# Moving the operands of TensorE's products to another place in SBUF: 192 bytes, by 256, from the stationary ones

## The chip, the cores and the metric

One core of a Trainium2 chip runs the whole model: TensorE (matmul), VectorE, ScalarE, GpSimd and SyncE (DMA queue), with SBUF (128 partitions of on-chip memory) and PSUM (where products add up). The metric is the device time of one execution in microseconds, the median of several runs.

## What is computed

Two transformer layers, then one block of another kind, on 256 tokens of 1024 features, in float32. Cut to its dense products, the reference is:

```python
x = x + concat(attention(h), mamba2(h)) @ out_w          # h = rmsnorm(x) @ in_w, split
x = x + (silu(h @ w_gate) * (h @ w_up)) @ w_down         # swiglu, D_FF = 2816
x = x + (gate_b * causal_conv(gate_c * v)) @ out_w       # short convolution, 1024 wide
x = x + (silu(h @ w_gate) * (h @ w_up)) @ w_down
x = rmsnorm(x)
x = x + (sigmoid(ga) * (y_a @ w_a) + sigmoid(gb) * (y_b @ w_b)) @ w_out   # second block
x = x + peer_ffn(rmsnorm(x), wq, sub_keys, u, v)
# peer_ffn: per token and head the 16 best of 128 x 128 experts; hid = gelu(u[expert] . x) * gate; sum of hid * v[expert]
```

The kernel computes `peer_ffn` densely: the hidden values of all 16384 experts (`u`, 128 chunks), a mask of gates, and the sum over all of them (`v`, 128 chunks).

## The kernel before

**Weights.** All weights come from HBM as a stream of 537 chunks of 128x1024 float32 (`Stream`): SyncE loads `raw` (three buffers), ScalarE writes its rounded part `whi` and VectorE the rest `wlo` (`cut`, lines 75 and 76), four buffers each, at most three chunks ahead of TensorE. The activations are split in the same way: `hh` and `hl` are h, and each stage has such a pair of its own (`yh` and `yl` and so on, by `split2`).

**Products.** One dense product is three instructions with the same output (`mm3`, lines 283 to 285), high by high, high by low, low by high. Each reads a stationary 128x128 tile, loaded into the array ahead of it, and a moving operand of 256 or 512 columns. In the profile's names the moving operand stands first: `w<-hh,whi` has hh moving and whi stationary. `gemm_b` has a chunk stationary and h moving, 24 products for one output; `gemm_o` has a chunk stationary and a pair y moving, each product of three going to the next of eight outputs; `gemm_a` has h stationary and the chunk moving, 512 columns wide as a rule.

**Stages, in order of time.** `mixer0` (the first 190 us), `ffn`, `short_conv`, `ffn`, `mixer2` (from about 660 us to 880), `peer` (the rest). In `peer` the products with `u` (`gemm_b`, to about 1290 us) run beside the search for the 16 best on VectorE and then beside one half of the gates (products of 64 columns, line 1616); the last stage, 128 chunks of `v`, runs beside the other half. There `part` splits two 128-row blocks of the hidden values at a time into h's own memory, and h is stationary. Between stages `enter` writes h anew. Work of VectorE and ScalarE that is not due at once stands in a list (`later`), and `run` issues it between the products, by credits, so its order on each engine is fixed when the program is written.

**Places in SBUF.** A place is an address within a partition; "by 256" is its remainder. Tiles lie one behind the other in the order of the pools: constants, the stream (raw, whi, wlo), `res` (xT, hh, hl), small, and each stage's own pool, in steps of 32 bytes. Before the change:

| tile | used by | place | by 256 |
|---|---|---|---|
| whi, wlo (four each, 4096 apart) | all | 31200, 47584 and on | 224 |
| xT | all | 63968 | 224 |
| hh, hl | all | 72160, 80352 | 224 |
| yah, yal | mixer0 | 203104, 207200 and on | 96 |
| ybh, ybl | mixer0 | 219552, 223648 and on | 160 |
| yh, yl | the first ffn | 108672, 112768 and on | 128 |
| yh, yl | short_conv | 110784, 115904 and on | 192 |
| yh, yl | the second ffn | 120960, 125056 and on | 128 |
| yah, ybh, mgh and their low parts | mixer2 | 207232, 203136, 215424 and on | 128 |

Within a tile, the blocks that a product reads lie 512 or 1024 bytes apart, so a product's remainder is its tile's. Moving less stationary, by 256, is then: h against the stream 0, in either role; mixer0's ya 128 (96-224) and yb 192; the FFNs' y 160; the short convolution's y 224; mixer2's ya, yb and mg 160. SBUF is nearly full: the highest place in use is 228063 of 229376.

Of the kernel before, what the change touches and what calls it, by code (L numbers as in the profile page):

```python
# [7 lines left out]
F32 = mybir.dt.float32  # L8
F32R = mybir.dt.float32r
# [109 lines left out]
class Kernel:  # L119
# [30 lines left out]
    def start(self):  # L150
        nc = self.nc
        c = self.const
        self.xT = self.res.tile([128, 8, 256], F32, name="xT")
        self.cols = self.a["cols"]
        self.g = c.tile([128, self.a["gains"].shape[1]], F32, name="gains")
        nc.scalar.dma_start(self.g, self.a["gains"])
        self.after = nc.scalar.dma_start(self.xT[:, 0:2], self.a["xT"][:, 0:2]).ins
        self.ones = c.tile([128, 128], F32, name="ones")
        nc.vector.memset(self.ones, 1.0)
        with self.tc.issue_after(self.after):  # L160
            a = nc.scalar.activation(c.tile([128, 1], F32, name="first"), self.ones[:, 0:1], AF.Copy)
        jp = self.jp = c.tile([128, 128], I32, name="jp")
        nc.gpsimd.iota(jp, pattern=[[1, 128]], base=0, channel_multiplier=-1)
        self.ident = c.tile([128, 128], F32, name="ident")
        v = nc.vector.tensor_scalar(self.ident, jp, 0.0, None, op0=OP.is_equal)
        self.idle = self.side([128, 128])
        self.spin(12)
        self.after = a.ins, v.ins
# [47 lines left out]
            v.tensor_mul(t, t, a)  # L216
            v.scalar_tensor_tensor(y, t, 1.5, y, op0=OP.add, op1=OP.mult)

    def parts(self, name="h"):
        return (self.res.tile([128, 8, 256], F32R, name=name + "h"), self.res.tile([128, 8, 256], F32R, name=name + "l"))  # L220

    def add(self, accs):

# [213 lines left out]
    def short_conv(self, h):  # L437
        nc, w, st = self.nc, self.work, self.st
        rsb = accs = None
        ys = []  # L440
        ahead = None

        def banks(bank=self.bank):
            return bank([128, 2, 256]), bank([128, 256])

        for b in range(8):
            cv, gb = ahead or banks(self.side if b == 0 else self.bank)
            if b == 0:
                self.gemm_b3([(cv[:, 0], True), (cv[:, 1], False), (gb, True)], h)
                rs = self.held(self.stats)()  # L450
                ahead = banks()
                for i in range(2):
                    self.gemm_b(ahead[0][:, i], h, st.next(), i == 0)
                self.gemm_b(ahead[1], h, st.next(), True)
                rsb = self.held(lambda: self.bcast_rs(rs))()
                accs = self.accs()
            else:
                if ahead is None:
                    for i in range(2):
                        self.gemm_b(cv[:, i], h, st.next(), i == 0)  # L460
                    self.gemm_b(gb, h, st.next(), True)
                ahead = None
            u = w.tile([128, 258], F32, name="u")
            nc.gpsimd.memset(u[:, 0:2], 0.0)
            t = w.tile([128, 256], F32, name="t")
            nc.vector.tensor_mul(t, cv[:, 0], rsb)
            nc.gpsimd.tensor_mul(t, t, rsb)
            nc.vector.tensor_mul(u[:, 2:258], cv[:, 1], t)
            c = w.tile([128, 256], F32, name="c")
            self.conv(c, u, [self.col("l1_conv", 8 * k + b) for k in range(3)], None)  # L470
            g = w.tile([128, 256], F32, name="gb")
            nc.vector.tensor_mul(g, gb, rsb)
            nc.vector.tensor_mul(c, c, g)
            ys.append(self.split2(c, w, "y", [128, 256], 5))
            if b >= 3:
                self.gemm_o(accs, ys[b - 3], st.next(), b == 3, False)
        self.gemm_o(accs, ys[5], st.next(), False, False)
        self.gemm_o2(accs, ys[6:])
        return accs
# [27 lines left out]
    def mixer0(self, h):  # L507
        nc, w, st, a = self.nc, self.work, self.st, self.a
# [4 lines left out]
        def t1(shape, name, dtype=F32, bufs=1, tag=None):  # L513
            return w.tile(shape, dtype, name=name, tag=tag or name, bufs=bufs)
# [3 lines left out]
        p = self.side([128, 256])  # L518
# [16 lines left out]
        for i, f in enumerate((lambda k: key(k), lambda k: latent(c1, k), lambda k: key(k), lambda k: latent(c1, k),  # L535
                               lambda k: key(k), lambda k: key(k), lambda k: latent(c2, k), lambda k: latent(c2, k))):
            k = (0, 0, 2, 2, 4, 6, 4, 6)[i]
# [101 lines left out]
        self.run(1)  # L639


        cs = t1([128, 2, 256], "cs")
        for tb in range(2):
            S.activation(cs[:, tb], cps[tb], AF.Copy, scale=rs[:, tb:tb + 1])
        cn = (t1([128, 2, 256], "cnh", F32R), t1([128, 2, 256], "cnl", F32R))
# [97 lines left out]
        for b in range(2):  # L743
            p = wbank([128, 2, 256])
# [7 lines left out]
        for tb in range(2):  # L752
            p = wbank([128, 512])
# [124 lines left out]
        MM, yy = {}, {}  # L878
# [18 lines left out]
        def ssd(tb, g):  # L897
            def f():
                o = slice(512 * g, 512 * g + 512)
                p = self.side([128, 512])  # L900
                for j in range(2):
                    m = MM.pop((tb, g, j))
                    for i in range(4):
                        hh = 4 * j + i
                        T.matmul(p[:, hh * 64:hh * 64 + 64], m[:, i], xdt[:, tb, 512 * g + hh * 64:512 * g + hh * 64 + 64],  # L905
                                 start=True, stop=True)
                y = t1([128, 512], "yy", bufs=1)
                if tb:
                    p2 = self.side([128, 512])
                    T.matmul(p2, bcT[:, 2 + g, 128:256], state[:, g], start=True, stop=True)  # L910
                    V.tensor_tensor(y.rearrange("p (h d) -> p h d", d=64), p2.rearrange("p (h d) -> p h d", d=64),
                                    eacs[:, 8 * g:8 * g + 8][:, :, None].to_broadcast([128, 8, 64]), op=OP.mult)
                    V.tensor_add(xsd[:, tb, o], xsd[:, tb, o], y)
                V.tensor_add(xsd[:, tb, o], p, xsd[:, tb, o])
            return f
# [3 lines left out]
        def gate1(tb, g):  # L919
            def f():  # L920
                o = slice(512 * g, 512 * g + 512)
                y = xsd[:, tb, o]
                V.tensor_mul(y, y, zs[:, tb, o])
                sq = t1([128, 512], "ysq", bufs=1, tag="yy")
                S.activation(sq, y, AF.Square, accum_out=yss[:, g, tb:tb + 1])
            return f

# [69 lines left out]
        for k in range(12):  # L997
# [3 lines left out]
            y = yaT[k // 2] if k < 4 else ybT[(k - 4) // 2]  # L1001
# [461 lines left out]
    def peer(self, h, out):  # L1463
# [219 lines left out]
        for tb in range(2):  # L1683
            for k in range(8):
                T.matmul(accs[2 * tb + k // 4][:, k % 4 * 128:k % 4 * 128 + 128], self.xT[:, k, tb * 128:tb * 128 + 128], self.ident,
                         start=(k % 4 == 0), stop=False, is_transpose=True, skip_group_check=True)
        def part(b):
            s = 2 * b % 8
            x = hid[:, 2 * b:2 * b + 2]
            S.activation(h[0][:, s:s + 2], x, AF.Copy)  # L1690
            V.tensor_sub(h[1][:, s:s + 2], x, h[0][:, s:s + 2])  # L1691
# [158 lines left out]
```

## Time and profile before

| | |
|---|---|
| median of 3 runs | 1672.65 us (1672.6 to 1674.53) |
| the profiled execution | 1672.04 us |
| its span, first to last instruction | 1670.2 us |
| TensorE busy | 1657.0 us, 99% |
| VectorE busy | 1245.7 us, 75% |
| ScalarE busy | 834.0 us, 50% |
| read from HBM | 283.22 MB, 170 GB/s over the span |

TensorE's records overlap: a product of 256 columns is recorded with 0.28 us, but the next one starts some 0.12 us after it. What a product costs the engine is therefore the distance from its start to the next one's start, to be read from the timeline. The timeline's starts are rounded to 10 ns, so a distance is taken over many products: the last start less the first, by the number of steps.

### The profile page before, as it was taken

The numbers are of one execution on the slowest core, as the hardware profiler recorded it, in microseconds if no ns is written. First come the engines' busy times: TensorE is split into PE (matmuls) and PEld (weight loads), VectorE is DVE, ScalarE is ACT, GpSimd is POOL, SyncE is SP. The second block draws the span as 40 slices with busy tenths as digits, with TensorE's granted clock in tenths as the row PEclk, the third lists the DMA queues.
The fourth block names the chain that finished last, engine by engine and source line by source line (L and its number), as shares of the span: only waits on it lengthen the run. The fifth ranks groups of instructions, "written<-read, shape, count | busy, mean of one in ns | idle before, by whom it ended". The sixth has DMA issues, their size and how long they took to land.

```text
span 1670.2 us, 31492 instructions
## 1 busy us (share of the span) xinstructions
PE 1657.0 (99%) x12792; PEld 1552.7 (93%) x12792; DVE 1245.7 (75%) x2263; ACT 834.0 (50%) x1146; POOL 52.4 (3%) x79
## 2 busy tenths in 40 slices
PE   8999999999999999999999999999999999999999
PEld 8898999999999999888999999999999888888887
DVE  7988765668687557886478986978887889965553
ACT  6676544444454445655555454543434444444443
POOL 2000100002010001000001000000000000000000
PEclk9999999999999999999999999999999999999999
DMA  6334565555555554544354655464545555555554
GB/s 217 126 118 129 174 189 183 184 177 183 185 188 180 187 187 154 192 136 151 114 179 161 192 186 180 161 194 164 165 165 165 167 175 176 171 184 190 196 195 139
DMA packets 79601, 286.38 MB, mean 171 GB/s; under 512 B 8848, under 2 KB 9312, under 8 KB 79456
## 3 DMA queue, kind: packets, MB, share of 16 engines
q1 hardware_dynamic: 78912, 283.41, 51.8%
q8 instruction: 100, 1.64, 0.4%
q0 software_dynamic: 176, 0.55, 0.2%
q10 hardware_dynamic: 368, 0.41, 0.1%
q14 instruction: 45, 0.37, 0.1%
HBM read 283.22 MB, written 1.05 MB: 170 GB/s over the span
## 4 chain that ended last, share of the span: by engine, by line
PE 94%; DVE 4%; ACT 1%; issue 1%; DMA 1%; SPq 0%; DVEq 0%; ACTq 0%
PE w L283 18%; PE w L284 18%; PE w L285 18%; PE acc L283 11%; PE acc L285 11%; PE acc L284 11%; PE w L1616 2%; DVE wlo L76 2%; ACT whi L75 1%; DMA raw<-in_w_m_dram 1%; PE acc L1382 0%; PE acc L1344 0%; PE acc L905 0%; PE acc L1515 0%; PE acc L803 0%
## 5 line engine op out<-in xcount | busy, mean ns | idle before, releaser
L75 ACT ACTIVATE whi<-raw 128x1024 fp32r<-128x1024 f32 (+1 forms) x541 | 567.0, 1050 | 591.0 <-PE w L284 274.2
L76 DVE TENSOR_TENSOR wlo<-raw,whi 128x1024 fp32r<-128x1024 f32 (+1 forms) x541 | 659.6, 1222 | 228.0 <-ACT whi L75 225.9
L283 PE MATMUL w<-hh,whi 128*128 128x256 f32 x2216 | 634.7, 286 | 0.0
L284 PE MATMUL w<-hl,whi 128*128 128x256 f32 x2216 | 628.7, 284 | 0.0
L285 PE MATMUL w<-hh,wlo 128*128 128x256 f32 x2216 | 628.2, 284 | 0.0
L283 PEld LDWEIGHTS w<-hh,whi 128*128 128x128 f32 x2216 | 425.4, 192 | 2.6 <-issue 1.3
L285 PEld LDWEIGHTS w<-hh,wlo 128*128 128x128 f32 x2216 | 425.3, 192 | 0.8 <-issue 0.7
L284 PEld LDWEIGHTS w<-hl,whi 128*128 128x128 f32 x2216 | 425.6, 192 | 0.3
L283 PE MATMUL acc<-whi,hh 128*128 128x512 f32 (+1 forms) x528 | 207.6, 393 | 0.7 <-ACT whi L75 0.7
L285 PE MATMUL acc<-whi,hl 128*128 128x512 f32 (+1 forms) x528 | 204.5, 387 | 0.0
L284 PE MATMUL acc<-wlo,hh 128*128 128x512 f32 (+1 forms) x528 | 204.1, 387 | 0.3 <-DVE wlo L76 0.3
L285 PEld LDWEIGHTS acc<-whi,hl 128*128 128x128 f32 x528 | 99.2, 188 | 20.4
L284 PEld LDWEIGHTS acc<-wlo,hh 128*128 128x128 f32 x528 | 99.5, 188 | 19.8 <-DVE wlo L76 0.5
L283 PEld LDWEIGHTS acc<-whi,hh 128*128 128x128 f32 x528 | 99.4, 188 | 19.6 <-ACT whi L75 0.8
L283 PE MATMUL acc<-yh,whi 128*128 128x256 f32 x416 | 116.7, 281 | 0.0
L284 PE MATMUL acc<-yl,whi 128*128 128x256 f32 x416 | 116.6, 280 | 0.0
L285 PE MATMUL acc<-yh,wlo 128*128 128x256 f32 x416 | 116.6, 280 | 0.0
L1690 ACT ACTIVATE hh<-hid 128x512 fp32r<-128x512 f32 x64 | 40.3, 631 | 91.7 <-PE acc L284 91.4
L284 PEld LDWEIGHTS acc<-yl,whi 128*128 128x128 f32 x416 | 78.5, 189 | 0.0
L283 PEld LDWEIGHTS acc<-yh,whi 128*128 128x128 f32 x416 | 78.4, 189 | 0.0
L285 PEld LDWEIGHTS acc<-yh,wlo 128*128 128x128 f32 x416 | 78.4, 188 | 0.0
L1691 DVE TENSOR_TENSOR hl<-hid,hh 128x512 fp32r<-128x512 f32 x64 | 44.0, 691 | 33.8 <-ACT hh L1690 33.8
(459 smaller groups left out, 1988.7 us busy)
## 6 DMA issues: line engine op xcount, KB each, us to landing
raw<-in_w_peer_dram SPq DMA_DIRECT2D x264, 512.0 KB, 3.3
raw<-in_w_f_dram SPq DMA_DIRECT2D x132, 512.0 KB, 3.3
raw<-in_w_m_dram SPq DMA_DIRECT2D x106, 512.0 KB, 3.3
raw<-in_w_l_dram SPq DMA_DIRECT2D x32, 512.0 KB, 3.3
raw<-in_w_m_dram SPq DMA_DIRECT2D x5, 256.0 KB, 6.4
out_dram<-hid SPq DMA_DIRECT2D x4, 256.0 KB, 2.1
xT<-in_xT_dram SPq DMA_DIRECT2D x3, 256.0 KB, 6.3
hid<-in_peer_sk_dram POOLq DMA_DIRECT2D x1, 512.0 KB, 3.5
```

What stands on the lines that cost most here:

```text
L75: a = self.nc.scalar.activation(hi[:, s], r[:, s], AF.Copy)
L76: v = self.nc.vector.tensor_sub(lo[:, s], r[:, s], hi[:, s])
L283: t.matmul(out, l[0], r[0], start=start, stop=False, skip_group_check=True)
L284: t.matmul(out, l[0], r[1], start=False, stop=False, skip_group_check=True)
L285: self.hist.append(t.matmul(out, l[1], r[0], start=False, stop=stop, skip_group_check=True).ins)
L1616: T.matmul(p[:, i], x2[:, i], o1[ps][:, g % 2, j, i], start=(j == 0), stop=(j == 1))
L1690: S.activation(h[0][:, s:s + 2], x, AF.Copy)
L1691: V.tensor_sub(h[1][:, s:s + 2], x, h[0][:, s:s + 2])
```

## The change

xT, h, and some scratch tiles get a few bytes of room behind them (`roomy` allocates a longer tile and returns a view), so that what is allocated behind them lies at other places. xT gets 48 elements (192 bytes), hh 64 (256 bytes), hl 88 (352 bytes), `cs` 8 (32 bytes), `yy`/`ysq` 48 (192 bytes), and the two buffers of `u` go from 258 elements (1056 bytes in steps of 32) to 288 (1152). In the last stage h is another view of the same two tiles, `h2`, 32 elements (128 bytes) further on. No instruction is added or taken away.

```diff
     def start(self):
...
-        self.xT = self.res.tile([128, 8, 256], F32, name="xT")
+        self.xT = self.roomy([128, 8, 256], F32, "xT", 48)
...
-    def parts(self, name="h"):
-        return (self.res.tile([128, 8, 256], F32R, name=name + "h"), self.res.tile([128, 8, 256], F32R, name=name + "l"))
+    def roomy(self, shape, dtype, name, room, pool=None, at=0, **kw):
+
+        n = 1
+        for k in shape[1:]:
+            n *= k
+        x = (pool or self.res).tile([shape[0], n + room], dtype, name=name, **kw)[:, at:at + n]
+        return x if len(shape) == 2 else x.rearrange("p (a b) -> p a b", b=shape[2])
+
+    def parts(self):
+
+        x = [self.res.tile([128, 2048 + r], F32R, name=n) for n, r in (("hh", 64), ("hl", 88))]
+        self.h2 = [y[:, 32:2080].rearrange("p (k t) -> p k t", k=8) for y in x]
+        return [y[:, 0:2048].rearrange("p (k t) -> p k t", k=8) for y in x]
...
-            u = w.tile([128, 258], F32, name="u")
+            u = self.roomy([128, 258], F32, "u", 30, w)
...
-        cs = t1([128, 2, 256], "cs")
+        cs = self.roomy([128, 2, 256], F32, "cs", 8, w, bufs=1)
...
-                y = t1([128, 512], "yy", bufs=1)
+                y = self.roomy([128, 512], F32, "yy", 48, w, bufs=1)
...
-                sq = t1([128, 512], "ysq", bufs=1, tag="yy")
+                sq = self.roomy([128, 512], F32, "ysq", 48, w, bufs=1, tag="yy")
...
+        h = self.h2
+
         def part(b):
```

## Rows read from the trace of the kernel before

**Rows 1.** The page: busy time and share of each engine; TensorE's granted clock.

```profile
PE 1657.0 (99%) x12792; PEld 1552.7 (93%) x12792; DVE 1245.7 (75%) x2263; ACT 834.0 (50%) x1146; POOL 52.4 (3%) x79
...
PEclk9999999999999999999999999999999999999999
```

**Rows 2.** Stretches: from:to, length, each engine's busy us (x instructions), clock, DMA.

```profile
40.00:160.00 120.00, 118.54 (x865) 105.19 (x865) 105.30 (x264) 85.93 (x167) 0.42 (x4) 1.00 0.40 128
200.00:640.00 440.00, 440.00 (x3696) 440.00 (x3696) 296.85 (x424) 206.58 (x280) 20.91 (x32) 1.00 0.56 185
...
920.00:1120.00 200.00, 200.00 (x1685) 199.24 (x1684) 169.93 (x460) 95.30 (x112) 0.00 (x0) 1.00 0.58 183
1290.00:1480.00 190.00, 190.00 (x1289) 155.23 (x1288) 166.24 (x253) 83.65 (x96) 0.00 (x0) 1.00 0.52 172
```

**Rows 3.** Groups by form, TensorE: out<-moving,stationary, shapes, count, busy us, mean ns, idle.

```profile
L283 PE MATMUL w<-hh,whi 128*128 128x256 f32 x2216 | 634.7, 286 | 0.0
...
L283 PE MATMUL acc<-whi,hh 128*128 128x512 f32 x512 | 202.9, 396 | 0.0
...
L283 PE MATMUL acc<-yh,whi 128*128 128x256 f32 x416 | 116.7, 281 | 0.0
...
L283 PE MATMUL w<-whi,hh 128*128 128x512 f32 x112 | 45.0, 401 | 0.0
...
L283 PE MATMUL acc<-hh,whi 128*128 128x256 f32 x128 | 36.6, 286 | 0.0
...
L283 PE MATMUL w<-ybh,whi 128*128 128x256 f32 x80 | 22.4, 280 | 0.0
...
L283 PE MATMUL w<-yah,whi 128*128 128x256 f32 x64 | 18.3, 285 | 0.0
...
L283 PE MATMUL acc<-mgh,whi 128*128 128x256 f32 x64 | 18.0, 281 | 0.0
```

**Rows 4.** Timeline (start us, us), first and last of 95 products, relation 0.

```profile
233.60 0.28 PE L283 MATMUL w<-hh,whi 128*128 128x256 f32 x1
...
244.87 0.28 PE L284 MATMUL w<-hl,whi 128*128 128x256 f32 x1
```

**Rows 5.** Timeline, first and last of 14 products of mixer0, relation 128.

```profile
155.86 0.28 PE L284 MATMUL w<-yal,whi 128*128 128x256 f32 x1
...
157.41 0.28 PE L285 MATMUL w<-yah,wlo 128*128 128x256 f32 x1
```

**Rows 6.** Timeline, first and last of 95 products of an FFN, relation 160.

```profile
362.26 0.28 PE L283 MATMUL acc<-yh,whi 128*128 128x256 f32 x1
...
373.29 0.28 PE L284 MATMUL acc<-yl,whi 128*128 128x256 f32 x1
```

**Rows 7.** Timeline, first and last of 95 products of the short convolution, relation 224.

```profile
454.84 0.28 PE L283 MATMUL acc<-yh,whi 128*128 128x256 f32 x1
...
465.97 0.28 PE L284 MATMUL acc<-yl,whi 128*128 128x256 f32 x1
```

**Rows 8.** Timeline, first and last of 107 products of mixer0, relation 192.

```profile
170.88 0.28 PE L283 MATMUL w<-ybh,whi 128*128 128x256 f32 x1
...
182.90 0.28 PE L284 MATMUL w<-ybl,whi 128*128 128x256 f32 x1
```

**Rows 9.** Timeline, first and last of 178 products, 512 columns, last stage, relation 0.

```profile
1519.70 0.39 PE L284 MATMUL acc<-wlo,hh 128*128 128x512 f32 x1
...
1559.82 0.39 PE L284 MATMUL acc<-wlo,hh 128*128 128x512 f32 x1
```

**Rows 10.** A stretch of 20 us in the search for the 16 best.

```profile
1080.00:1100.00 20.00, 20.00 (x169) 20.00 (x168) 20.00 (x13) 9.87 (x12) 0.00 (x0) 1.00 0.54 172
```

**Rows 11.** Waits, 920 to 1120 us: who waited for whom, us in total, times, longest.

```profile
ACT whi L75 <- PE w L284: 64.1, 40, 3.1
```

**Rows 12.** Groups by form, VectorE, 200 to 390 us (first FFN).

```profile
L504 DVE TENSOR_TENSOR yl<-sg,yh 128x256 fp32r<-128x256 f32 x22 | 9.3, 425 | 9.2 <-ACT yh L503 9.2
```

**Rows 13.** Groups by form, VectorE, 400 to 470 us (short convolution).

```profile
L504 DVE TENSOR_TENSOR yl<-c,yh 128x256 fp32r<-128x256 f32 x8 | 3.3, 419 | 0.5 <-ACT yh L503 0.5
```

## The prediction, made blind

> **What bounds the kernel now.** I read the page first: TensorE is busy for 99% of the span at a granted clock of 1.0 in every slice, while VectorE has 75% and ScalarE 50% [rows 1]. Then the table by stretch: from 200 to 640 us, 920 to 1120 and 1290 to 1480 TensorE is busy for the whole stretch, VectorE for 67, 85 and 87% of it [rows 2]. So the time is a number of products times the distance from one product's start to the next's. The mean durations of the groups do not give that distance, because products overlap in the records: 2216 products of 286 ns on one line alone [rows 3], 634.7 us, would not fit three times into the span. The distance has to be taken from starts in the timeline, and that is where the case lies.
>
> **The price of a place, read from the kernel before.** "Relation" is the place of the moving operand less that of the stationary one, by 256 bytes. The table in the kernel's section gives it for every dense product, and there are five of them in this one kernel. At relation 0, h moving: 233.60 to 244.87 us is 94 steps, 11.27 us, 119.9 ns a step [rows 4]. At 128, the first mixer's attention part: 155.86 to 157.41, 13 steps, 119.2 ns [rows 5]. At 160, an FFN's second product: 362.26 to 373.29, 94 steps, 117.3 ns [rows 6]. At 224, the short convolution's: 454.84 to 465.97, 94 steps, 118.4 ns [rows 7]. At 192, the first mixer's ybh and ybl: 170.88 to 182.90, 106 steps, 113.4 ns [rows 8]. All five are 256 columns against a 128x128 stationary tile with the same weight loads, and four of them run in the same form of loop, with the same stream of splits beside them. The 512-column products of the last stage, at relation 0: 1519.70 to 1559.82, 177 steps, 226.7 ns [rows 9]. The last and the first differ by 106.8 ns for 256 more columns, one column a cycle at 2.4 GHz, so 13.1 ns of each step at relation 0 do not depend on the columns; at 192 the same sum leaves 6.6 ns. The price of relation 0 against 192 is 119.9 less 113.4, 6.5 ns a product. Why a step should depend on it (the next product's weights are read while the moving operand of this one is) the trace does not show; that it goes with the place I take from the five rows.
>
> Against this speaks a rule of the Trainium skill, "TensorE: Matmul & The Clock Gate", Part 2, step 1: the engine has two independent read ports, and "Loading the next tile's weights doesn't steal SBUF read bandwidth from the running matmul." By it the place could not matter and the sum would be 0; 113.4 against 119.9 ns in the same form speaks against it, and it is a rival below.
>
> **The change part by part.** It adds and removes no instruction; places move and nothing else. By the sizes in the diff xT keeps its place, hh and hl move by 192 and 448 bytes and by 192 by 256 both, everything behind them by 800, so by 32; what lies behind cs in the first mixer by 32 more, behind yy by 192 more; in the short convolution two u buffers add 96 each, 192.
>
> First, h moving against the stream's chunks: relation 0 to 192 (2216 and 128 of each of three products, 7032 in all [rows 3]) at 6.5 ns [rows 4, 8]: 45.7 us.
>
> Second, the other moving operands. The FFNs' yh, yl: 160 to 192, 352 of the 416, so 1056 products at 3.9 ns: 4.1 us. The short convolution's 64: 224+32+192 is again 192, 192 products at 5.0 ns: 1.0 us. The gated mg (64): 192 products at 3.9: 0.7 us. yah: 32 at 128 and 32 at 160, 96 products at 5.8 and 96 at 3.9: 0.9 us. ybh: 64 of the 80 stay at 192 (+32+32+192 is 256), 16 come from 160: 0.2 us. Together 7.0 us [rows 3, 5 to 8].
>
> Third, the last stage: h stationary, the chunk moving. With h2, 128 bytes further, the chunk at 224 less h2 at 32 is 192: 512 of each of three, 1536 products [rows 3]. No row shows 512 columns at 192. One end is nothing, the other is all of the 13.1 ns (20.1 us); a loss I exclude because 0 is the slowest of the five relations. I take 6.5 ns, since the part of the step that does not depend on the columns is the same 13.1 ns for both widths: 10.0 us.
>
> Fourth, the dense products with h stationary outside the last stage go from 0 to 64, which no row shows: 112 of each of three, 336 products [rows 3], between a loss and a gain of 6.5 ns, 2.2 us either way; I take half the gain, since every relation but 0 is below 0's 119.9: 1.1 us. Some 200 more, in smaller groups, are left out.
>
> The sum is 45.7+7.0+10.0+1.1 = 63.8 us of TensorE's steps.
>
> **What of it reaches the end.** VectorE and ScalarE keep their instructions. In 200 to 640 us they have a third of the time and more to spare, so all of it counts. In 920 to 1120, TensorE would need 200 x 113.4/119.9 = 189 us, VectorE has 170 us of work; in 1290 to 1480 it has 166 us against 190 less some 5. Between, single slices are full: VectorE is busy 20.00 of 20 us from 1080 to 1100 [rows 10], where the top-16 search runs, and TensorE's 20 us become 18.9. A lag of about 1 us is taken up by the three chunks of splits ahead: ScalarE waited 64.1 us there for TensorE to free a buffer [rows 11], so the stream runs up against its limit and not behind. I take off 2.2 us for this and the hand-overs from stage to stage, where h is written by the other engines and nothing there gets shorter. In the first mixer VectorE has 105.3 of 120 us from 40 to 160, and TensorE's 865 instructions [rows 2] can win 5.6 us at most; its turn there is set by chains through both, so I take off half, 2.8 us. Covers gone wholly would cost these two twice, 5 us more. Net: 63.8-5.0 = 58.8 us.
>
> The profiled execution took 1672.04 us, 1.84 more than its span of 1670.2, and the median is 0.6 above it. 1672.04-58.8 = 1613.2, and with 0.6 the median is 1614. The new slot h2 overlaps the old h by all but its ends, so the first part of the last stage waits for the same last products of the stage before; I cost it at nothing, covered by the 16 transposes that TensorE runs there, and at the time of one product, 0.1 us, otherwise.
>
> **Rivals.** (a) It is the moving operand's own place that counts (160 by 256, where ybh lies), not the relation. For: stationary tiles lay at 224 in all five rows, so these cannot tell the two apart. Then all but the last stage comes out the same, since h moves to 160 too, and the last stage's chunks, moving at 224 as before, win nothing: 1614+10 = 1624. (b) h gets only what the other places give: its loop accumulates in one place for 24 products, and no row shows that loop at 192. At the price of the yh row, 2.6 ns, the first term is 18.3 us, the second stays at 7.0 and the third is 4.0; less 5.0, 24.3 us: 1648. Against it: the rows of gemm_o at 128 and gemm_b at 0 are within 0.7 ns of each other. (c) No effect: the 113.4 ns belong to that stage and not to the place, or a tile does not land where I reckon. 1672. (By the rule of the Trainium skill, "TensorE: Matmul & The Clock Gate", Part 2, step 1, the result is this one.) Against it: the row at 128 stands 14 us earlier in the same loop. (d) Slower: VectorE pays for its operands' new places, which move by 32 or more in all background work. It sets the pace where it now has 336 of 390 us (920 to 1120, 1290 to 1480); TensorE would need some 374 there, so it decides from 11% more on, and eats all of the gain from 29% (434 us). With a third more, 447 us, the time is 1614+73 = 1687. Against it: yl is written in 425 ns at place 128 and in 419 at place 192 [rows 12, 13].
>
> **How the numbers follow.** The forecast has 0.75, (a) 0.10, (b) 0.06, (c) 0.05, (d) 0.04. Its own range: without anything taken off, with the fourth term at its end and half as much again in the last stage, 1614-5-1-5 = 1603; with what is taken off doubled, the fourth term a loss and (a), 1614+5+3+10 = 1632, of which I keep 1630. The range 1602 to 1630 takes in the forecast and (a), and leaves out (b), (c), (d) and a little more, under 2 in 10. About 0.2%, 3.3 us, is what a measurement of this kernel can tell from no change; faster by more than that 0.91, within it 0.05, slower 0.04.
>
> **What would show it.** The first step is right if the timeline has h's products 113 to 114 ns apart in an FFN, and wrong if they stay near 120 or stop at 117. The third is right at 220 ns in the last stage; at 226.7 it is (a). VectorE's share should rise to 77%, with the same busy time; if its busy time grows it is (d). If TensorE's idle time grows in the first mixer or near 1080 us by more than 5 us, the part taken off was too small.

## The result and the profile after

| | before | after |
|---|---|---|
| median | 1672.62 us | 1655.05 us (1653.5 to 1658.48, 4 runs) |
| ratio, 95% interval | | 0.9896 (0.9878 to 0.9914) |
| the profiled execution, its span | 1672.04, 1670.2 us | 1653.5, 1651.7 us |

The change makes the kernel 17.6 us faster, 1.0%. The forecast was 58.8 us and 1614; the time lies above the whole range of 1602 to 1630. The direction was right and the size was not.

The page of after, first TensorE's line of busy time, then its granted clock (before: [rows 1]):

```profile
PE 1637.4 (99%) x12792; PEld 1522.2 (92%) x12792; DVE 1244.9 (75%) x2263; ACT 834.3 (51%) x1146; POOL 53.3 (3%) x79
...
PEclk9999999999999999999999999999999999999999
```

The same number of products, the same clock, VectorE's work unchanged (1244.9 against 1245.7 us), and TensorE busy for 99% of a shorter span. So the bound is the same, and the difference lies in the distances between products. Three stretches of after by engine, as in [rows 2] (from:to, length, busy us and instructions of PE, PEld, DVE, ACT, POOL, clock, DMA share, GB/s):

```profile
40.00:160.00 120.00, 117.95 (x869) 104.16 (x868) 105.62 (x264) 85.96 (x167) 0.42 (x4) 1.00 0.39 128
200.00:640.00 440.00, 440.00 (x3745) 439.99 (x3745) 301.54 (x430) 208.96 (x284) 20.93 (x32) 1.00 0.58 187
...
1290.00:1480.00 190.00, 190.00 (x1221) 151.25 (x1217) 159.72 (x235) 81.90 (x94) 0.00 (x0) 1.00 0.52 172
```

In 440 us of the feed-forward stages TensorE issues 3745 products where it issued 3696, 1.3% more and not 5%. From 1290 to 1480 us it issues 1221 where it issued 1289. That count holds narrow products too, and in before the window begins 8.6 us ahead of the last stage, so it only shows where to look; the starts give the sizes. First and last of 98 products in a row in the first FFN, at relation 192 (columns: start us, us, engine, line, operation; before, at relation 0: [rows 4]):

```profile
209.77 0.28 PE L296 MATMUL acc<-yh,wlo 128*128 128x256 f32 x1
...
221.20 0.28 PE L294 MATMUL w<-hh,whi 128*128 128x256 f32 x1
```

11.43 us over 97 steps are 117.8 ns, not 113.4. First and last of 98 products of the same form and relation in `peer`, at 940 and at 983 us:

```profile
939.73 0.28 PE L294 MATMUL w<-hh,whi 128*128 128x256 f32 x1
...
950.72 0.28 PE L295 MATMUL w<-hl,whi 128*128 128x256 f32 x1
...
982.75 0.28 PE L296 MATMUL w<-hh,wlo 128*128 128x256 f32 x1
...
994.18 0.28 PE L294 MATMUL w<-hh,whi 128*128 128x256 f32 x1
```

113.3 ns, and 43 us later in the same stage 117.8 ns. At one relation there are two lengths. And the last stage, first and last of 178 products of 512 columns (before: [rows 9]):

```profile
1514.65 0.39 PE L296 MATMUL acc<-whi,hl 128*128 128x512 f32 x1
...
1555.95 0.40 PE L296 MATMUL acc<-whi,hl 128*128 128x512 f32 x1
```

41.30 us over 177 steps, 233.3 ns, where before had 226.7. The last stage became slower.

Where the time went by stage, from the start of the same product in each trace (us; the lines of two experiments are used further on). The lines are drawn where long runs begin, so `mixer0` here holds the first 6 us of the FFN, and `mixer2` the first 50 us of `peer`:

```
         mixer0   ffn  conv    ffn  mixer2  peer: to the 16 best, beside them, beside gates  last stage
before    196.1 189.5  92.6  175.3   271.0               90.9        128.5           148.4       367.5
after     195.4 187.1  91.1  173.5   265.9               88.0        122.9           142.0       376.0
kick      194.5 181.1  88.6  167.6   267.5               89.3        123.7           142.0       367.7
best      196.9 181.0  88.5  167.4   267.2               87.1        123.2           142.5       367.7
```

After wins some 26 us in all stages but the last, most of it in `mixer2` and `peer`, and gives 8.5 us back in the last.

How one length turns into the other is seen at the start of the first FFN in after. Four narrow products for the norm stand between two unbroken runs (runs in which each product follows the one before without a gap); the run ahead of them goes by 113.3 ns (200.27 to 200.50 is two steps of 0.115), the run behind by 117.8 to its end 172 us later:

```profile
200.27 0.28 PE L294 MATMUL w<-hh,whi 128*128 128x256 f32 x1
200.38 0.28 PE L295 MATMUL w<-hl,whi 128*128 128x256 f32 x1
200.50 0.28 PE L296 MATMUL w<-hh,wlo 128*128 128x256 f32 x1
200.61 0.61 PE L428 MATMUL acc<-rsd,ones 128*128 128x128 f32 x4
200.98 0.36 PE L294 MATMUL w<-hh,whi 128*128 128x256 f32 x1
201.18 0.28 PE L295 MATMUL w<-hl,whi 128*128 128x256 f32 x1
```

I went through every unbroken run of dense products in the trace. At relation 192 nearly every run of 256 columns settles on 340 ns for three products or on 353, within a few products of its start, and keeps that to its end. Between, only an interruption (another instruction on TensorE, or a wait) changes it. Which of the two lengths a run takes is called its draw below. The three longest runs, 1466 products from 201 us, 650 from 388 and 1465 from 479, all stand behind such a group of four and all keep 117.8. That is 3581 products at 4.45 ns, 15.9 us.

A run whose relation the change left alone shows the second length too. In `mixer0` ybh and ybl stand at 192 in both kernels, in two runs of 71 and 118 products. In before both runs settle on 113.3 ns; in after the longer one does, and the other stands at 117.8, behind the same kind of narrow products. First and last of those 71, before and then after, 7.95 and 8.25 us over 70 steps:

```profile
160.29 0.28 PE L284 MATMUL w<-ybl,whi 128*128 128x256 f32 x1
...
168.24 0.28 PE L285 MATMUL w<-ybh,wlo 128*128 128x256 f32 x1
...
159.79 0.28 PE L295 MATMUL w<-ybl,whi 128*128 128x256 f32 x1
...
168.04 0.28 PE L296 MATMUL w<-ybh,wlo 128*128 128x256 f32 x1
```

So the trace of before, which has no other products at 192, showed one of the two lengths only.

### The profile page after: what moved, and what is told of

Read it like the earlier page. It is cut to its first block, busy times and chain, and to the rows that moved or that the text cites. A ratio compares the mean times of both kernels' runs of the same rounds, so it can differ in the third digit from the quotient of the medians.

```text
span 1651.7 us, 31492 instructions
## 1 busy us (share of the span) xinstructions
PE 1637.4 (99%) x12792; PEld 1522.2 (92%) x12792; DVE 1244.9 (75%) x2263; ACT 834.3 (51%) x1146; POOL 53.3 (3%) x79
## 4 chain that ended last, share of the span: by engine, by line
PE 86%; DVE 10%; ACT 1%; DMA 1%; issue 1%; SPq 0%; DVEq 0%; ACTq 0%
PE w L294 16%; PE w L296 15%; PE w L295 15%; PE acc L294 11%; PE acc L296 11%; PE acc L295 11%; DVE wlo L76 4%; PE w L1627 2%; DMA raw<-in_w_m_dram 1%; DMA raw<-in_w_peer_dram 1%; ACT whi L75 1%; PE acc L1393 0%; PE acc L1355 0%; PE acc L916 0%; DVE hid L1513 0%
## 5 line engine op out<-in xcount | busy, mean ns | idle before, releaser
L294 PE MATMUL w<-hh,whi 128*128 128x256 f32 x2216 | 624.6, 282 | 0.0
L296 PE MATMUL w<-hh,wlo 128*128 128x256 f32 x2216 | 618.5, 279 | 0.6 <-DVE wlo L76 0.6
L295 PE MATMUL w<-hl,whi 128*128 128x256 f32 x2216 | 618.4, 279 | 0.1
L296 PEld LDWEIGHTS w<-hh,wlo 128*128 128x128 f32 x2216 | 420.3, 190 | 2.5 <-DVE wlo L76 1.5
L294 PEld LDWEIGHTS w<-hh,whi 128*128 128x128 f32 x2216 | 417.0, 188 | 2.7 <-issue 1.3
L295 PEld LDWEIGHTS w<-hl,whi 128*128 128x128 f32 x2216 | 417.3, 188 | 0.6 <-DVE hl L1663 0.3
```

Of the source, the lines that this page charges most:

```text
L294: t.matmul(out, l[0], r[0], start=start, stop=False, skip_group_check=True)
L295: t.matmul(out, l[0], r[1], start=False, stop=False, skip_group_check=True)
L296: self.hist.append(t.matmul(out, l[1], r[0], start=False, stop=stop, skip_group_check=True).ins)
```

## The experiments

Two theories stood against each other. Theory H: the relation sets the distance, and at 192 it has two lengths that are held from one interruption to the next. Its rival, S: the length belongs to the stage, that is to the work of the other engines beside it (the stream's writes and reads of SBUF, the splits), and the relation has little to do with it.

**1. Bare products (`probe`).** The model is left out. One chunk is loaded and copied to places of eight relations; then TensorE alone runs 48 products for each relation, behind one of three interruptions, first with 256 columns (the copy moving), then with 512 (the copy stationary):

```python
def stop(kind):      # 0: float32, 128 columns; 1: four float16 of 64 columns; 2: float32, 1 column
...
for f in (w256, w512):
    for kind in range(3):
        for r in (0, 32, 64, 96, 128, 160, 192, 224):
            stop(kind)
            f(r, 16)      # 16 times the three products of mm3
```

> This kernel leaves out the whole model: one weight chunk and eight copies of it at relations 0, 32, ... 224, and then only dense products, 48 in a run at each relation, each run begun by one of three interruptions (a float32 product of 128 columns, four float16 products of 64, a float32 product of one column), then runs at 0 followed by 36 products at each other relation without a break; all of it with 256 columns and again with 512. Nothing else runs beside them. Theory H (held): at relation 192 the distance between products is either 113.3 or 117.8 ns with 256 columns and is held through an unbroken run from its first products on; at 0 every run settles at 119.9. With 512 columns 192 gives 233.3 and 0 gives 226.7. Rival S (stage): the 117.8 ns of the FFNs and the 233.3 ns of the last stage come from what the other engines do there or from the kernel's other places; then here 192 gives 113.3 in every run, and 512 columns at 192 give 220.

Measured. Relation 192, 42 products behind the float32 interruption and 42 behind the four of float16; then 43 products of 512 columns at relation 0 and 44 at 192:

```profile
45.76 0.28 PE L64 MATMUL acc<-hh,whi 128*128 128x256 f32 x1
...
50.59 0.28 PE L66 MATMUL acc<-hh,wlo 128*128 128x256 f32 x1
...
92.74 0.28 PE L64 MATMUL acc<-hh,whi 128*128 128x256 f32 x1
...
97.39 0.28 PE L66 MATMUL acc<-hh,wlo 128*128 128x256 f32 x1
...
204.75 0.39 PE L65 MATMUL acc<-wlo,hh 128*128 128x512 f32 x1
...
214.28 0.39 PE L65 MATMUL acc<-wlo,hh 128*128 128x512 f32 x1
...
272.79 0.39 PE L65 MATMUL acc<-wlo,hh 128*128 128x512 f32 x1
...
282.82 0.40 PE L66 MATMUL acc<-whi,hl 128*128 128x512 f32 x1
```

4.83 us and 4.65 us over 41 steps, 117.8 and 113.4 ns: both lengths of the kernel, with nothing beside TensorE. Of 512 columns, 9.53 us over 42 steps and 10.03 over 43: 226.9 and 233.3. So S falls: nothing of a stage is needed for either length. By the programs' addresses the stationary tiles of this loop lie at 128 by 256 and the moving ones of relation 192 at 64; in after they lie at 224 and 160. The same relation with both places different has the same two lengths, so it is the relation that counts and neither place alone. The settled lengths of all runs of this and the two later probes, from the second half of each (several values: several runs):

```
relation    256 columns, ns            512 columns, ns
0           120.0                      226.7 (all nine runs)
16          113.3, 118.7               226.7 (one run)
32          116.7, 117.8               233.3
64          113.3 or 117.8             228.9
96          120.0                      233.3
112         113.3 (all)                226.7 or 233.2 to 233.5
128         118.5 to 120.0             232.1 to 232.8
160         117.2 to 118.8             234.2
192         113.3 or 117.8             233.3 (all)
224         118.3                      233.3
48, 80, 144, 176, 208, 240             116.7 to 120.0     229.7 to 233.3
odd multiples of 8                     118.5 to 122.2     226.7 to 233.3
```

No run of 256 columns settled below 113.3 and none of 512 below 226.7. Relation 192 is as good as any for 256 columns if the draw is good; with 512 it was slower than 0 in every run.

**2. The changed kernel once more (`after_again`),** to see whether the three long runs always draw 117.8.

> The changed kernel once more, unaltered. Theory H: each of the three long unbroken runs (first FFN, short convolution, second FFN) is at 113.3 or at 117.8 ns from end to end; if the draw at a run's start depends on its exact timing, one of them can differ from the first profile, and the time by 6.5 ns-steps of some us: 1650 to 1659. Rival S: the same three stages stand at 117.8 again, and the time within 1 us of 1653.5.

1658.39 us, one execution. The three runs stand at 117.8 again. But now the run in `peer` that had 113.3 at 940 us does too:

```profile
939.72 0.28 PE L296 MATMUL w<-hh,wlo 128*128 128x256 f32 x1
...
951.15 0.28 PE L294 MATMUL w<-hh,whi 128*128 128x256 f32 x1
```

11.43 us over 97 steps. In this execution the runs from 897 to 1030 us and the one from 1078 us stand at 117.8, 1329 products; in the first one 236 of the products in this stretch did, most of them from 977 to 1003 us. The 1093 more at 4.45 ns make 4.9 us of steps. The two executions differ by 4.9 us, but 0.9 of that stands already at the start of the first long run (202.12 us against 201.18), and of the steps some 4.0 us reach the end, by the stages. So the draw makes most of this difference, by what these two traces show: behind the four narrow products at the start of a long run it falls the same way each time, in `peer`, where TensorE now and then waits for a split, it doesn't.

**3. The last stage back at relation 0 (`last0`).** One line of after is changed; all else keeps its place.

```diff
-        self.h2 = [y[:, 32:2080].rearrange("p (k t) -> p k t", k=8) for y in x]
+        self.h2 = [y[:, 16:2064].rearrange("p (k t) -> p k t", k=8) for y in x]
```

> The second place of h in the last stage lies 64 bytes behind the first instead of 128, so that its relation is 0 as before the change; nothing else differs. Theory H (the relation sets the distance, and 192 is worse than 0 at 512 columns): the last stage is at 226.7 ns again, 1536 products x 6.6 = 10.1 us less, 1645. Rival S (the loss in the last stage is from the second view as such, overlapping h): 233 ns stays and 1655.

1645.92 us (1644.68 to 1647.18), ratio 0.9837 (0.982 to 0.9853). First and last of 178 products of the last stage:

```profile
1514.73 0.39 PE L296 MATMUL acc<-whi,hl 128*128 128x512 f32 x1
...
1554.85 0.39 PE L296 MATMUL acc<-whi,hl 128*128 128x512 f32 x1
```

40.12 us over 177 steps, 226.7 ns as before the change, and the kernel is 9.1 us faster than after. So 192 in the last stage cost time, and a second place of h as such did not. The moving operand, the chunk, has the same place (224) in before, after and `last0`; only the stationary one moved. So it isn't the moving operand's own place that counts.

**4. An interruption in the long runs (`kick`).** `last0`, and in each FFN and the short convolution, early in the long run, four float16 products of zeros are added to the output (12 instructions in all). Their tile of zeros moves everything behind it by 256 bytes, which leaves every relation as it was.

```diff
+    def kick(self, out):
+        for _ in range(4):
+            self.nc.tensor.matmul(out[:, 0:64], self.zero, self.zero[:, 0:64], start=False, stop=False, skip_group_check=True)
...
+            if kick and k == 0:
+                self.kick(out)
```

> The version with the last stage at relation 0, and in each FFN and in the short convolution, once, four float16 products of 64 columns with zeros, added to the output that is being summed, after the third dense product of a chunk: an interruption of the kind after which the bare products at 192 stood at 113.3 ns. Theory H: from there to the end of each stage the products stand 113.3 ns apart instead of 117.8, about 1440+600+1440 products x 4.45 ns = 15.5 us less than 1645.9 less some 0.6 us for the interruptions: 1631. Rival S (the FFNs' other work makes the 117.8): 117.8 stays, 1646.

1633.82 us (1632.0 to 1634.27), ratio 0.9762 (0.9746 to 0.9778): 12.1 us less than `last0`, with more instructions. The start of the first FFN, and 97 products of it later on:

```profile
200.78 0.29 PE L322 MATMUL w<-zero 128*128 128x64 f16 x4
200.90 0.36 PE L296 MATMUL w<-hh,whi 128*128 128x256 f32 x1
...
209.83 0.28 PE L296 MATMUL acc<-yh,whi 128*128 128x256 f32 x1
...
220.71 0.28 PE L296 MATMUL w<-hh,whi 128*128 128x256 f32 x1
```

10.88 us over 96 steps, 113.3 ns, in the same stage with the same stream beside it; all three long runs keep it. In the table by stage the first FFN, the convolution and the second FFN are 6.0, 2.5 and 5.9 us shorter than in after. This is what separates H from S within the kernel itself. It brought 12.1 us where 15.9 were to be had: the three stretches won 14.4, and the draw in `peer` and in `mixer2` fell worse in this execution. From 882 to 1014 us its runs stand at 117.8, and the table's `mixer2` and the first part of `peer` are 2.9 us longer than in after.

**5. The same interruptions in the kernel before (`before_kick`).**

> The kernel before with the same three interruptions and nothing else. Theory H: at relation 0 h's products settle at 119.9 ns whatever interrupts them; the time is that of before plus 0.5 to 1 us, 1673. Rival S2 (interruptions alone shorten the steps, the relation has no part): the FFNs fall below 119.9 and the time by up to 15 us.

1671.59 us, one execution, no difference. 98 products of the first FFN at relation 0:

```profile
232.82 0.28 PE L287 MATMUL acc<-yh,wlo 128*128 128x256 f32 x1
...
244.44 0.28 PE L285 MATMUL w<-hh,whi 128*128 128x256 f32 x1
```

119.8 ns. At relation 0 the interruptions change nothing, so the gain of `kick` needs the relation as well: one that has a shorter length to fall into.

**6. More relations, and ten interruptions at 192 (`probe2`).** The model is left out again. Eleven more relations; the high and the low part of h at different relations; and at 192 ten kinds of interruption, twice each.

> Leaves out the whole model, as the first bare run did: products alone, in runs of 24 to 48. Relations in odd steps of 16 bytes, high and low part of h at two different relations, and at 192 ten kinds of interruption, each twice. Theory H: at 192 each kind of interruption gives 113.3 or 117.8, the same both times and held to the run's end; where high and low part lie at different relations one of which is 0, the distance lies between, and no run is below 113.3. Rival (the state is drawn by chance): the two runs of one kind differ. With 512 columns no relation but 0 is at 226.7 or below.

The relations are in the table above. High and low part at different relations gave 117.2 to 120.0, never 113.3. Of the kinds of interruption I had hoped for one that always gives 113.3, and none can be named. Nine of the ten gave the same length both times; one, four float32 records in a row, gave 117.75 and then 113.3. And a kind does not carry over from one program to the next: behind the float32 interruption relations 64 and 192 drew 113.3 here where `probe` drew 117.8, and behind four of float16 relation 64 drew 117.8 where `probe` drew 113.3. At 192 the length of the run before was often carried over an interruption: one of float16 with 128 columns set it to 117.8, and it stayed there through the float32 ones until the next of float16. What sets the draw is open. But 112 gave 113.3 both times.

**7. Everything at 112 (`v112`).** h, the blocks' products and the last stage go to 112, the products with h stationary outside the last stage to 144. In `mixer0` yb stays at 192, and ya goes to 64. The places of the blocks' operands are moved by more lines of the same kind.

```diff
-        self.xT = self.roomy([128, 8, 256], F32, "xT", 48)
+        self.xT = self.roomy([128, 8, 256], F32, "xT", 24)
...
-        self.h2 = [y[:, 32:2080].rearrange("p (k t) -> p k t", k=8) for y in x]
-        return [y[:, 0:2048].rearrange("p (k t) -> p k t", k=8) for y in x]
+        self.h2 = [y[:, 12:2060].rearrange("p (k t) -> p k t", k=8) for y in x]
+        return [y[:, 4:2052].rearrange("p (k t) -> p k t", k=8) for y in x]
...
-        hi = w.tile([128, 2, 256], F32R, name=name + "h", bufs=bufs)
+        hi = self.roomy([128, 2, 256], F32R, name + "h", self.room, w, self.room // 16, bufs=bufs)
```

> The changed kernel with other places: h against the chunks, the FFNs', the short convolution's and the second mixer's moving operands at relation 112 instead of 192, the last stage at 112 too, no added interruption. In the bare products 112 stood at 113.3 ns after both kinds of interruption with 256 columns (it got there by itself within some ten products) and at 226.7 with 512. Theory H (a relation has lengths that it holds and others that it leaves; 112 holds only the shortest): every long run at 113.3 in every stage, the top-16 stretch of the last block too; 7100 products of h x 6.6 = 46.8 us, y and mg some 5, the 336 wide ones outside the last stage, now at 144, lose 6.6 each, 2.2; against 1672.7 that is 1623, less what the stretches with VectorE full give back (2 to 5): 1625 to 1628. Rival (the two states at 192 come from the interruption alone and belong to no relation): 112 shows 117.8 in the FFNs as 192 did, 1640 or more.

1640.19 us (1639.96 to 1641.81), ratio 0.9804 (0.9788 to 0.982); the expectation missed by 12 us or more, and the time is the one that the rival named, but not by the rival's cause. Every long run of 256 columns at 112 settles on 113.3, in the FFNs and in `peer` as well, and the executions lie within 1.9 us. But the last stage, 177 products:

```profile
1514.61 0.40 PE L296 MATMUL acc<-wlo,hh 128*128 128x512 f32 x1
...
1555.67 0.40 PE L295 MATMUL acc<-whi,hh 128*128 128x512 f32 x1
```

41.06 us over 176 steps, 233.3 ns. One run of 512 columns in `probe2` had settled on 226.7 at 112, and I had built on it.

**8. Is 112 settled? (`probe3`).** The model is left out. Relation 112 behind the ten kinds of interruption with 256 columns; 0 and 112 behind six of them with 512; the odd multiples of 8.

> Leaves out the whole model, as the other bare runs did. Relation 112 after ten kinds of interruption, each twice, and after 0 and 192 without a break; the relations at odd multiples of 8 bytes; 512 columns at 0 and 112 after six kinds. Theory H: at 112 every run ends at 113.3 with 256 columns and at 226.7 with 512, whatever came before; at 0 with 512 every run ends at 226.7. Rival: some kinds leave 112 at 117.8 or above. No theory says what the odd multiples of 8 give; below 113.3 or 226.7 none is expected.

With 256 columns all twenty runs of 24 products at 112 end at 113.3, and so do the two behind unbroken products at 0 and at 192; it takes up to 15 products to get there, and the runs of 12 behind a float32 interruption end at some 117 before they do. With 512 columns, 0 stands at 226.7 behind all six; 112 at 233.2 to 233.5 behind five and at 226.7 behind one, eight float16 products. 33 products behind a single float16 one and 33 behind the eight:

```profile
447.28 0.40 PE L67 MATMUL acc<-whi,hh 128*128 128x512 f32 x1
...
454.74 0.40 PE L69 MATMUL acc<-whi,hl 128*128 128x512 f32 x1
...
481.74 0.39 PE L67 MATMUL acc<-whi,hh 128*128 128x512 f32 x1
...
488.99 0.39 PE L69 MATMUL acc<-whi,hl 128*128 128x512 f32 x1
```

7.46 and 7.25 us over 32 steps. So 112 is for 512 columns what 192 is for 256: two held lengths. The miss of `v112` lies in this: its last stage held the longer one.

**9. 112 for 256 columns, 0 for the last stage (`best`).** `v112` with h2 moved on.

```diff
-        x = [self.res.tile([128, 2048 + r], F32R, name=n) for n, r in (("hh", 64), ("hl", 24))]
-        self.h2 = [y[:, 12:2060].rearrange("p (k t) -> p k t", k=8) for y in x]
+        x = [self.res.tile([128, 2048 + r], F32R, name=n) for n, r in (("hh", 64), ("hl", 88))]
+        self.h2 = [y[:, 40:2088].rearrange("p (k t) -> p k t", k=8) for y in x]
```

> The kernel v112 with the second place of h moved once more, so that the last stage's moving operand stands at relation 0 to h (v112: 112); everything else keeps its relation: 112 for h and the blocks' products, 144 for the products with h stationary outside the last stage. Theory H (relation alone sets the length: 112 settles at 113.3 ns for 256 columns, 0 at 226.7 ns for 512): the last stage's 1536 products fall from about 233.3 to 226.7 ns, 1536 x 6.6 = 10.1 us, so 1640.2 - 10.1 = 1630 us (1627 to 1633), with the two feed-forward stretches and the short convolution unbroken at 113.3 as in v112 and with executions that lie within some 2 us. Rival D (the last stage of v112 was long by a draw of its own and not by its relation): 1640 with 512 columns still near 233. Rival B (the shorter last stage is taken back by a wait behind it, as the loading of its weights): 512 columns at 226.7, but the time above 1635 and waits of TensorE for weights in the last stage.

1632.09 us (1631.44 to 1633.31, 5 runs), ratio 0.9753 (0.974 to 0.9766): 41.3 us faster than before and 23 faster than the change. Its page, 97 products of the first FFN, 98 of `peer`, 178 of the last stage:

```profile
PE 1614.9 (99%) x12790; PEld 1506.3 (92%) x12792; DVE 1244.9 (76%) x2263; ACT 834.4 (51%) x1146; POOL 53.5 (3%) x79
```

```profile
209.81 0.28 PE L297 MATMUL w<-hh,wlo 128*128 128x256 f32 x1
...
220.69 0.28 PE L297 MATMUL w<-hh,wlo 128*128 128x256 f32 x1
...
969.80 0.28 PE L295 MATMUL w<-hh,whi 128*128 128x256 f32 x1
...
980.79 0.28 PE L296 MATMUL w<-hl,whi 128*128 128x256 f32 x1
...
1514.71 0.39 PE L295 MATMUL acc<-whi,hh 128*128 128x512 f32 x1
...
1554.83 0.39 PE L295 MATMUL acc<-whi,hh 128*128 128x512 f32 x1
```

113.3, 113.3 and 226.7 ns. It is 8.1 us faster than `v112`, a little less than the 10.1 expected: each short block of the last stage begins with nine longer products, so that the mean there falls from 233.3 to 227.7 and not to 226.7. It and `kick` come within 2 us of each other by different ways, and `best` needs no luck in `peer`.

## Why the prediction was wrong

I took the mean step of every dense product that another follows without a gap (more than 25 ns above the columns at 2.4 GHz counts as a gap), over the whole of both traces:

```
products, columns            before   after    best   count   won by after, us
h moving, 256                119.82  115.37  113.84    7032     31.3
y of FFNs and conv, 256      117.52  117.77  113.33    1248     -0.3
mg, 256                      118.62  113.38  113.56     192      1.0
ya, 256                      118.41  114.08  115.46     192      0.8
yb, 256                      114.36  114.67  114.67     240     -0.1
last stage, 512              227.58  233.23  227.71    1536     -8.7
h stationary, else, 512      228.26  229.76  233.29     336     -0.5
h stationary, else, 256      119.77  117.20  119.91     192      0.5
```

The sum is 24.0 us where the prediction had 63.8. The profiled executions differ by 18.5, so 5.5 us did not reach the end.

The step that failed is the price of relation 192. The prediction took it as one number, the same sign for both widths and the same length every time. It was wrong in the third term (a loss at 512 columns, which the prediction excluded) and in the first two (a second, longer length at 256 columns). Either alone puts the time outside the range: 1614+18.7 = 1633 and 1614+14.4+5.6 = 1634. Term by term:

- **What bounds the kernel** was right. TensorE issues product upon product, at a granted clock of 1.0 throughout, and the price is the distance of starts.
- **That the distance goes with the relation** was right, and the probe shows it without the kernel. The Trainium skill, "TensorE: Matmul & The Clock Gate", Part 2, step 1, says that loading the next tile's weights doesn't steal read bandwidth from the running product. What the prediction drew from it for its rival (c), that the place could not matter, does not hold: bare products take 120.0 ns at relation 0 and 113.3 at 112, and here the measurement decides. That the reads of the two get in each other's way is a guess that fits; no run shows it.
- **First term, h: 45.7 forecast, 31.3 measured.** That the relation sets the price was right, its size was off. The 113.4 ns of [rows 8] is one of two lengths at 192, and I took it for the only one. It stood on 107 products of one run, to be multiplied by 7032; the other run at 192 in before stands at 113.3 too, so the second length could not be read from that trace. The three long runs drew it. Rival (b) named a smaller price for h, and its 1648 came nearest, but by luck: its reason, the loop that accumulates in one place, is wrong, since the same loop runs at 113.3 in `peer` of after and in the FFNs of `kick`.
- **Second term: 7.0 forecast, 1.4 measured.** For the same reason: the y products stand in the same unbroken runs as h, so they drew 117.8, which is no better than the 117.3 they had [rows 6]. mg and ya won 1.8 us, about what was forecast for them (1.6); yb, whose relation hardly changed, lost 0.1 by the draw.
- **Third term, the last stage: a gain of 10.0 forecast, a loss of 8.7 measured.** This is the largest error of one term, 18.7 us, and what failed is the sentence "a loss I exclude because 0 is the slowest of the five relations". The five relations were read at 256 columns. At 512 no relation tried was faster than 0, and 192 is among the slowest. That the part of the step that doesn't depend on the columns is the same for both widths was an assumption: at 0 it is 13.3 ns for both, but at 192 it is 113.3-106.7 = 6.7 ns or 11.1 for 256 columns and 233.3-213.3 = 20.0 for 512. A range that allowed a loss of the size of the gain, 20 us from the value that I took, with what was added for the taken-off part and the fourth term, would have reached 1614+20+5+3 = 1642, and still not 1655.
- **Fourth term: 1.1 forecast, -0.5 measured,** within its bounds of 2.2. The 256-column products that were left out won 0.5.
- **What was taken off: 5.0 forecast, 5.5 measured.** The size is in part luck, as it was reckoned for a larger gain. In the first mixer the steps won 2.7 us, where the prediction allowed 5.6, and the stage became 0.7 us shorter, so some 2.0 were lost there (2.8 forecast). Some 2 more were lost in the two stretches of `peer` ahead of the gates, and 1.4 in the table's `mixer2`, for which nothing was taken off but the hand-overs. From 920 to 1120 us TensorE now waits for splits, where it waited for nothing before, and ScalarE's waits for TensorE to free a buffer fell from 64.1 [rows 11] to 52.2 us (47.3 in the row below, 4.9 behind another line). Waits of that stretch in after (who waited for whom, us in total, times, longest):

```profile
ACT whi L75 <- PE w L295: 47.3, 31, 3.0
...
PEld w L296 <- DVE wlo L76: 1.5, 5, 0.5
...
PE w L296 <- DVE wlo L76: 0.6, 2, 0.3
```

These waits are short, but a wait is an interruption too: behind one of 0.17 us for a split, at 977 us, the run of 113.3 ns goes on at 117.8.

- **The rivals.** (a), with 1624, was the case in which the last stage wins nothing; its reason, the moving operand's own place, falls with `last0`. (c), no effect, falls. (d), VectorE slower, falls: its busy time is unchanged, and yl took 424 and 419 ns where it took 425 and 419 [rows 12, 13]. What was missing is a rival in which the width changes the order of the relations, and one in which a relation has more than one length.

## What to carry to other kernels

A price that is read from one stretch of a trace may be one of several that the same work can have. Look at every stretch of that form before it is multiplied by thousands; here even that would have shown one length only, so where a form is rare in the trace, run it in a bare loop behind several interruptions. A price read at one width is not carried to another with its sign. Where dense products with a new stationary tile each stand back to back, try the relation of the two operands' places by 256 bytes in a bare loop, for each width, and take one that settled on the short length behind every interruption tried (112 for 256 columns and 0 for 512 here) and not one that sometimes does.

## What the runs showed of the hardware

- Back-to-back float32r products with a new 128x128 stationary tile each settled, at a granted clock of 1.0, on a length that depends on the relation of the two places in SBUF: 256 columns on 113.3 to 122.2 ns, 512 on 226.7 to about 234.
- At some relations there are two lengths that are held for as long as the run isn't broken: 113.3 and 117.8 ns at 192 and 64 with 256 columns (at 192 some 1460 products in a row at 113.3 in `kick` and at 117.8 in after), 226.7 and 233.3 at 112 with 512. An interruption can change the length, or carry it over. At 112 with 256 columns and at 0 with 512 every run that was long enough fell back to the short one, within some 15 products.
- The order of the relations turns with the width: 0 is among the slowest for 256 columns (120.0), and for 512 (226.7) none was faster.
- Open: what in an interruption decides the length (its kind alone did not: the same kind drew either length), why 112 settles and 192 doesn't, and which reads collide.
